# Hybrid attention, retention and ConvFFN layer on one core: early up-projection products re-ordered and placed in free half banks, reads and stores moved to other tiles and another queue

## The chip, the core and the metric

The kernel runs on one core of a Trainium2 chip. The metric is the time of one execution on the device in microseconds (us). Before the change three runs gave 1783.08, 1786.04 and 1786.34 us, median 1786.04. The engines are called as the profile calls them: PE is TensorE's matmul (PEld its weight load), DVE is VectorE, ACT is ScalarE, POOL is GpSimd and SP is SyncE, which here only issues DMAs. Each engine works its own instructions strictly in the order in which they stand; semaphores tie the engines together.

## The reference

One layer of a diffusion backbone over 1024 latent tokens of width 1024 and 256 context tokens. Attention and retention branches are merged and projected by `w_out` into a gated residual; a gated MLP with a depthwise convolution over tokens follows. The change touches the seam between the two:

```python
x = x + g1 * _merge(o_na, o_ret, xga, xgb, w_proj_na[l], w_proj_ret[l], w_out[l])
hx2 = _modulate(_rmsnorm(x, norm2_g[l]), sh2, sc2)
x = x + g2 * _conv_ffn(hx2, w_up[l], conv_w[l], conv_b[l], w_down[l])
...
return _rmsnorm(x, final_norm_g)

def _conv_ffn(h, w_up, conv_w, conv_b, w_down):
    u = h @ w_up
    ...
```

## The kernel before

**Precision.** Every float32 operand is split into a high and a low part (`split`, lines 85 to 87: a cast on ACT, then a subtraction on DVE), and a product is three matmuls: high with high, high with low, low with high (`open3`, L1374).

**Output projection.** `out_proj(tb)` makes the 128 tokens of one token block tb, 0 to 7: 48 matmuls into two PSUM tiles `om`, gate and residual on DVE (L1642, L1643), a store of the row block into `d_x1` (L1644), the squares on ACT (L1646), a scaling of their sum on DVE (L1647), a power on POOL (L1648) and the normed rows `xn` on DVE (L1649). `norm_out(tb)` transposes `xn` by 128-column pieces on TensorE (L1663), modulates them on ACT (L1670, L1673) and DVE (L1674, L1675). The normed tokens go into `h2`: the first half of the tokens into `h2a`, the second into `h2h` and `h2l`. For blocks 0 to 3 the modulated block `v` is also stored in `d_h` (L1677); for blocks 4 to 7 that store of the block 4 earlier is read back into `vo` (L1659), four differences are formed (L1681 to L1684) and, but for block 7, stored in `d_t` (L1689). Block 7's differences are split straight into the operands `T1` to `T4`.

**Up-projection.** It is a multiplication scheme with seven block products in place of eight (`Seven`). The weights of one unit n (one of 22) are the four blocks a11, a12, a21, a22, and POOL forms four sums of them, s1 to s4 (L1388 to L1391). The moving operands are halves of `h2` (B11, B21, B22) and the differences T1 to T4. Each unit has four half tiles of PSUM, each 128x512: `self.X`, `self.Y` and `self.Z` for the results, and a fourth, the second half of the tile z, that is not used. `u_tile` hands out tiles of two such halves.

**The seam.** Two units (`EARLY`) start before all tokens are normed. `early_plain(n)` makes a11 with B11 in X, copies X to p1 (L1718, on ACT), and adds a12 with B21 in X, which is C11, a block of the result. Then `norm_out(7)` follows, whose two transposed halves go into both halves of the tile z of unit 0, then reads of the twelve stored differences from `d_t` into `ur` tiles (`ur_load`, L1738) and their splits into T1 to T4. The `ur` tiles are twelve, and the weights `w_up` of all units and their sums s1 to s4 use the same twelve. `open` copies C11 out of X (`c11`, L1839, on ACT) and multiplies s4 with B22 into the same X; `close` makes the products with T1 to T4 and adds.

**What sets the order.** The text of the kernel gives the data flow; a scheduler lays each engine's instructions in a row. All loads of this stage, and all its stores, are issued on SP's queue. Tiles of a pool are handed on when their last reader is done. The pool `gates0` behind `gtile(0, ...)` has 17 tiles of 128x512, which held operands of the projections of the first token half; p1 and the other temporaries of the up-projection come from it.

Of the kernel before, what the change touches and what calls it, by code (L numbers as in the profile page):

```python
# [8 lines left out]
F32 = mybir.dt.float32  # L9
F32R = mybir.dt.float32r  # L10
AF = mybir.ActivationFunctionType
ALU = mybir.AluOpType
# [28 lines left out]
def tile_hybrid_layer(ctx, tc: tile.TileContext, io, dbg=None):  # L41
# [1519 lines left out]
    def gtile(half, dt, name):  # L1561
        return gpool[half].tile([P, 512], dt, tag="g", bufs=2 * KB + 1, name=name)
# [67 lines left out]
    def out_proj(tb):  # L1630
        half, ts = tb // 4, slice((tb % 4) * P, (tb % 4 + 1) * P)
        x1 = op.tile([P, D], F32, tag="x1", bufs=2, name="x1")
        xr = op.tile([P, D], F32, tag="xn", bufs=2, name="xn")
        sync.dma_start(x1, io["x"][tb * P : (tb + 1) * P])
        for dh in range(2):
            cs = slice(dh * 512, dh * 512 + 512)
            m = po.tile([P, 512], F32, tag="o", bufs=2, name="om")
            for kb in range(KB):
                wc = wo[kb, dh]
                h_, l_ = mg[kb, half]  # L1640
                mm3(m, h_[:, ts], l_[:, ts], wc[:, 0], wc[:, 1], kb == 0, kb == KB - 1)
            vec.tensor_tensor(xr[:, cs], m, gate1[:, cs], ALU.mult)  # L1642
            vec.tensor_tensor(x1[:, cs], xr[:, cs], x1[:, cs], ALU.add)  # L1643
        sync.dma_start(d_x1[tb * P : (tb + 1) * P], x1)  # L1644
        ss = op.tile([P, 2], F32, tag="ss", bufs=2, name="ss")
        act.activation(xr, x1, AF.Square, accum_out=ss[:, 0:1])  # L1646
        vec.tensor_scalar(ss[:, 0:1], ss[:, 0:1], 1.0 / D, EPS, ALU.mult, ALU.add)  # L1647
        pool.tensor_tensor(ss[:, 1:2], ss[:, 0:1], mhalf[:, 0:1], ALU.pow)  # L1648
        vec.tensor_scalar(xr, x1, ss[:, 1:2], None, ALU.mult)  # L1649
        return xr  # L1650

    def norm_out(tb, xr, banks=None):
        half, ts = tb // 4, slice((tb % 4) * P, (tb % 4 + 1) * P)
        if tb == 4:
            h2[1] = [None] * KH + [(gtile(0, F32R, "h2h"), gtile(0, F32R, "h2l")) for _ in range(KH)]
        vr = op.tile([P, KB, P], F32, tag="v", bufs=2, name="v")
        if half:
            vo = op.tile([P, KB, P], F32, tag="vo", bufs=1, name="vo")
            sync.dma_start(vo, d_h[tb - 4])  # L1659
        for kg in (1, 0):  # L1660
            tp = banks[kg].rearrange("p (k t) -> p k t", k=4) if banks else po.tile([P, 4, P], F32, tag="t", bufs=2, name="tp2")
            for k in range(4):
                pe.transpose(tp[:, k], xr[:, (kg * 4 + k) * P : (kg * 4 + k + 1) * P], ident)  # L1663
            for k in range(4):
                kb = kg * 4 + k
                t = h2[half][kb]
                a, sh = a2[:, kb : kb + 1], col[:, 24 + kb : 25 + kb]
                v = vr[:, kb]
                if t is None:
                    act.activation(v, tp[:, k], AF.Identity, bias=sh, scale=a)  # L1670
                    continue
                h_, l_ = (t[:, 0, ts], t[:, 1, ts]) if half == 0 else (t[0][:, ts], t[1][:, ts])
                act.activation(h_, tp[:, k], AF.Identity, bias=sh, scale=a)  # L1673
                vec.tensor_scalar(v, tp[:, k], a, sh, ALU.mult, ALU.add)  # L1674
                vec.tensor_tensor(l_, v, h_.bitcast(F32), ALU.subtract)  # L1675
        if half == 0:
            sync.dma_start(d_h[tb], vr)  # L1677
            return

        (b11, b21), (b12, b22) = [(t[:, :KH], t[:, KH:]) for t in (vo, vr)]  # L1680
        vec.tensor_tensor(b11, b12, b11, ALU.subtract)  # L1681
        vec.tensor_tensor(b12, b22, b12, ALU.subtract)
        vec.tensor_tensor(b22, b22, b11, ALU.subtract)
        vec.tensor_tensor(b21, b21, b22, ALU.subtract)  # L1684
        for c, t in enumerate((b11, b22, b12, b21)):
            if banks:
                split(combs[f"T{c + 1}"][0][:, tb - 4], combs[f"T{c + 1}"][1][:, tb - 4], t)
            else:
                sync.dma_start(d_t[c, tb - 4], t)  # L1689

    xr = None
    for tb in range(NTB):
# [12 lines left out]
    def early_bank(n):  # L1705
        return u_tile(2 * n), u_tile(2 * n + 1)

    def early_prod(bank, n, i):
        w = wload(io["w_up"][seq[n], 0, i])
        for k in range(KH):  # L1710
            x = h2[0][i * KH + k]
            open3(bank, w[:, 0, k * P : (k + 1) * P], w[:, 1, k * P : (k + 1) * P], x[:, 0], x[:, 1], i == 0 and k == 0, i == 1 and k == KH - 1)

    def early_plain(n):
        X = early[n][0][:, 0:512]
        early_prod(X, n, 0)
        p1 = gtile(0, F32, "pu")
        act.copy(p1, X)  # L1718
        early_prod(X, n, 1)
        return p1  # L1720

    early, early_p1, combs = [early_bank(0)], [], {}
    early_p1.append(early_plain(0))
    po.release()
    pu.append(ps("u_ps1", "left"))
    wop.release()
    gpool[1].release()
    early.append(early_bank(1))
    early_p1.append(early_plain(1))


    rp = sb("raws", "right")
# [3 lines left out]
    def ur_load(src):  # L1736
        t = rp.tile([P, 512], F32, tag="r", bufs=12, name="ur")
        sync.dma_start(t, src)  # L1738
        return t
# [47 lines left out]
    class Up(Seven):  # L1787
# [17 lines left out]
        def open(self):  # L1805
            self.banks()
            self.p1 = early_p1[self.n]
            self.c11()
            self.prod(self.X, self.s4, "B22", True, True)

        def close(self, n):
            if n == 0:
                self.prod(self.Z, self.s1, "T1", True, True)
            elif n == 1:
                self.u2, self.u3 = (self.tmp() for _ in range(2))
                self.prod(self.Y, self.s2, "T2", True, False)
                vec.tensor_tensor(self.u2, self.Y, self.p1, ALU.add)
                vec.tensor_tensor(self.u2, self.X, self.u2, ALU.add)
                self.add(0, 1, self.Z, self.u2)
            elif n == 2:  # L1820
                self.prod(self.Y, self.s3, "T3", False, False)
                vec.tensor_tensor(self.u3, self.Y, self.p1, ALU.add)
                self.add(1, 1, self.Z, self.u3)
            else:
                self.prod(self.Y, self.a22, "T4", False, True)
                self.add(1, 0, self.Y, self.p1)
# [31 lines left out]
    units[0].load()  # L1858
    for c in ("T1", "T2", "T3", "T4"):
        combs[c] = [tpl.tile([P, 4, KH, P], F32R, name=f"{c}{i}") for i in range(2)]  # L1860
    norm_out(NTB - 1, xr, (early[0][1][:, 0:512], early[0][1][:, 512:1024]))
    for c in (0, 1, 2, 3):
        hi, lo = combs[f"T{c + 1}"]
        for b in range(3):
            raw = ur_load(d_t[c, b])
            split(hi[:, b], lo[:, b], raw.rearrange("p (k t) -> p k t", k=KH))
    op.release()
    tap = sb("conv", "right")
# [252 lines left out]
```

## Time and profile before

| what | us |
|---|---|
| median of three runs | 1786.04 |
| the profiled execution's own time | 1782.43 |
| its span, from first to last instruction | 1780.0 |
| PE busy in the span | 1722.8 |
| DVE busy | 1309.6 |
| ACT busy | 853.6 |
| POOL busy | 581.7 |

All the profile's times are of the one profiled execution, which took 1782.43 us, and count from its first instruction. In a row of the timeline stand the start, how long it took, engine, line, operation, output and inputs and how many such instructions follow each other; in brackets, how long the engine stood idle before it and who ended the wait. A row of the waits has in total, times, longest. In rows of DMA issues stands the median time from issue to landing.

### The profile page before, as it was taken

What the parts mean: (1) busy time and instruction counts of PE and PEld (TensorE: products, weight loads), DVE (VectorE), ACT (ScalarE), POOL (GpSimd) and SP (SyncE); (2) the same over time, 40 slices, a digit from 0 to 9 for tenths busy, and PEclk for the clock granted to TensorE, in tenths of its full rate; (3) what the DMA queues carried; (4) which work ended last, traced back from release to release, by engine and by line L of the source; (5) the groups of instructions that cost most, each with busy time, mean ns of one, the idle gap of its engine ahead of it and who ended that gap; (6) DMA issues with size and microseconds to landing.
All of it is one profiled execution on the core that took longest, in us unless ns stands there. A gap on an engine that the chain in (4) does not pass through costs nothing.

```text
span 1780.0 us, 24636 instructions
## 1 busy us (share of the span) xinstructions
PE 1722.8 (97%) x8333; PEld 1427.2 (80%) x8333; DVE 1309.6 (74%) x2444; ACT 853.6 (48%) x1843; POOL 581.7 (33%) x485
## 2 busy tenths in 40 slices
PE   8799999999999999999999999699999999999997
PEld 3588888888888888788888888478888888788886
DVE  4978888765776766777664556789889989875755
ACT  4666666653443434443344334444444444554444
POOL 2510000002244343565413300346555555211444
PEclk9799999999999999999999999899999999999999
DMA  8133434433231212577658634522332333586754
GB/s 338 50 118 117 126 110 125 139 108 118 72 100 53 75 39 91 176 241 226 206 196 304 221 126 172 193 93 93 106 102 89 106 119 101 165 285 195 243 159 160
DMA packets 138973, 260.54 MB, mean 146 GB/s; under 512 B 15808, under 2 KB 28256, under 8 KB 138848
## 3 DMA queue, kind: packets, MB, share of 16 engines
q1 hardware_dynamic: 120928, 238.01, 40.9%
q10 hardware_dynamic: 17920, 20.98, 3.3%
q8 instruction: 65, 1.06, 0.2%
q14 instruction: 60, 0.49, 0.1%
HBM read 187.87 MB, written 68.44 MB: 144 GB/s over the span
## 4 chain that ended last, share of the span: by engine, by line
PE 44%; issue 5%; DVE 3%; POOL 3%; ACT 1%; DMA 1%; POOLq 0%; ACTq 0%; DVEq 0%; SPq 0%
PE u L1374 29%; PE y L1374 4%; PE om L121 2%; PE om L122 2%; PE om L123 2%; PE pr L111 2%; PE pr L110 2%; PE pr L112 2%; POOL x L1935 1%; PE pn L112 1%; PE pn L111 1%; PE pn L110 1%; DVE wc L87 1%; DVE ta L1763 0%; DVE at L1763 0%
## 5 line engine op out<-in xcount | busy, mean ns | idle before, releaser
L1374 PE MATMUL u<-T,wc 128*128 128x512 f32 x1056 | 248.5, 391 | 1.3 <-DVE pu L1416 0.8
L1374 PEld LDWEIGHTS u<-T,wc 128*128 128x128 f32 x1056 | 197.5, 188 | 46.1 <-ACT pu L1413 3.1
L1374 PE MATMUL y<-wc,ahl 128*128 128x512 f32 x924 | 210.6, 389 | 2.7 <-DVE wc L87 1.8
L1374 PEld LDWEIGHTS y<-wc,ahl 128*128 128x128 f32 x924 | 173.3, 188 | 39.6 <-DVE wc L87 2.5
L87 DVE TENSOR_TENSOR wc<-ur,wc 128x512 fp32r<-128x512 f32 x139 | 125.9, 908 | 65.0 <-ACT wc L86 65.0
L86 ACT CAST wc<-ur 128x512 fp32r<-128x512 f32 x139 | 86.3, 622 | 126.5 <-PE y L1374 72.0
L1374 PE MATMUL u<-h2a,wc 128*128 128x512 f32 x528 | 126.0, 393 | 4.1 <-ACT pu L1718 3.3
L111 PE MATMUL mm<-low,wc 128*128 128x512 f32 (+1 forms) x328 | 123.9, 378 | 0.0
L1374 PEld LDWEIGHTS u<-h2a,wc 128*128 128x128 f32 x528 | 99.7, 190 | 26.3 <-ACT pu L1718 3.7
L110 PE MATMUL mm<-hx,wc 128*128 128x512 f32 x264 | 107.4, 407 | 0.3 <-DVE vc L221 0.3
L112 PE MATMUL mm<-hx,wc 128*128 128x512 f32 x264 | 105.0, 398 | 0.0
L86 ACT CAST wc<-s 128x512 fp32r<-128x512 f32 x88 | 54.1, 621 | 103.7 <-PE u L1374 92.2
L87 DVE TENSOR_TENSOR wc<-s,wc 128x512 fp32r<-128x512 f32 x88 | 90.7, 1036 | 6.3 <-ACT wc L86 5.9
L1513 POOL TENSOR_TENSOR col<-col,bcol 128x32 f32<-128x32 f32 x1 | 0.2, 250 | 282.2 <-DVE aw L538 282.2
L123 PE MATMUL mm<-wc,low 128*128 128x512 f32 (+1 forms) x240 | 91.2, 380 | 0.0
L1374 PE MATMUL u<-hxT,wc 128*128 128x512 f32 x384 | 89.6, 389 | 0.0
L1374 PEld LDWEIGHTS u<-hxT,wc 128*128 128x128 f32 x384 | 72.1, 188 | 15.0
L87 DVE TENSOR_TENSOR wc<-raw,wc 128x512 fp32r<-128x512 f32 x88 | 66.1, 761 | 22.5 <-ACT wc L86 22.3
L121 PE MATMUL mm<-wc,hx 128*128 128x512 f32 x192 | 75.2, 392 | 0.6 <-ACT r L1105 0.6
L122 PE MATMUL mm<-wc,hx 128*128 128x512 f32 x192 | 75.2, 392 | 0.0
L1388 POOL TENSOR_TENSOR s<-ur 128x512 f32<-128x512 f32 x22 | 34.8, 1582 | 121.8 <-DVE wc L87 77.4
L1374 PE MATMUL u<-h2h,wc 128*128 128x512 f32 x176 | 60.9, 407 | 13.5 <-ACT uu L1839 9.7
(389 smaller groups left out, 4635.3 us busy)
## 6 DMA issues: line engine op xcount, KB each, us to landing
ur<-in_w_up SPq DMA_DIRECT2D x88, 256.0 KB, 2.8
ur<-d_a SPq DMA_DIRECT2D x77, 256.0 KB, 3.1
aw<-in_w_ada SPq DMA_DIRECT2D x32, 512.0 KB, 3.4
pj<-in_w_down SPq DMA_DIRECT2D x44, 256.0 KB, 4.7
d_w<-pj SPq DMA_DIRECT2D x44, 256.0 KB, 2.0
d_a<-sa SPq DMA_DIRECT2D x44, 256.0 KB, 2.0
ur<-d_w SPq DMA_DIRECT2D x44, 256.0 KB, 3.5
d_a<-at SPq DMA_DIRECT2D x33, 256.0 KB, 2.6
```

What stands on the lines that cost most here:

```text
L86: act.copy(hi, src)
L87: (lo_eng or vec).tensor_tensor(lo, src, hi.bitcast(F32), ALU.subtract)
L110: pe.matmul(out, wh, xh, start=k == 0, stop=False)
L111: pe.matmul(out, wh, xl, start=False, stop=False)
L112: pe.matmul(out, wl, xh, start=False, stop=k == n - 1)
L121: pe.matmul(out, ah, bh, start=first, stop=False)
L122: pe.matmul(out, ah, bl, start=False, stop=False)
L123: pe.matmul(out, al, bh, start=False, stop=last)
L1374: pe.matmul(out, a, b, start=first and n == 0, stop=last and n == 2, skip_group_check=True)
L1388: pin(pool.tensor_tensor(self.s1, self.a21, self.a22, ALU.add))
L1513: pool.tensor_tensor(col[:, 16:48], col[:, 16:48], bcol[:, 16:48], ALU.add)
L1935: pool.tensor_tensor(z, z, fg[:, gs(dh)], ALU.mult)
```

## The change

1. `d_x1`, `d_h` and `d_t` are stored by DMAs of ACT's queue instead of SP's.
2. `vo` becomes two half tiles from `gtile(0, ...)`, read by two DMAs of 256 KB instead of one of 512 KB.
3. `early_first(n)` makes only a11 with B11 and the copy to p1, for both units; the products of a12 with B21 follow in the program's text behind `norm_out(7)`.
4. `norm_out(7)` transposes into the first halves of the two units' tiles z, not into both halves of unit 0's.
5. `open` multiplies s4 with B22 into `self.W`, the idle second half of z, instead of X; `close` adds W instead of X.
6. The twelve reads of `d_t` go into tiles `tr` of `gtile(0, ...)` instead of `ur` tiles.

```diff
-        sync.dma_start(d_x1[tb * P : (tb + 1) * P], x1)
+        act.dma_start(d_x1[tb * P : (tb + 1) * P], x1)
...
         if half:
-            vo = op.tile([P, KB, P], F32, tag="vo", bufs=1, name="vo")
-            sync.dma_start(vo, d_h[tb - 4])
+            vo = [gtile(0, F32, "vo").rearrange("p (k t) -> p k t", k=KH) for _ in range(2)]
+            for i in range(2):
+                sync.dma_start(vo[i], d_h[tb - 4, :, i * KH : i * KH + KH])
...
-            sync.dma_start(d_h[tb], vr)
+            act.dma_start(d_h[tb], vr)
             return
-        (b11, b21), (b12, b22) = [(t[:, :KH], t[:, KH:]) for t in (vo, vr)]
+        (b11, b21), b12, b22 = vo, vr[:, :KH], vr[:, KH:]
...
-                sync.dma_start(d_t[c, tb - 4], t)
+                act.dma_start(d_t[c, tb - 4], t)
...
-    def early_plain(n):
-        X = early[n][0][:, 0:512]
-        early_prod(X, n, 0)
-        p1 = gtile(0, F32, "pu")
-        act.copy(p1, X)
-        early_prod(X, n, 1)
-        return p1
-
-    early, early_p1, combs = [early_bank(0)], [], {}
-    early_p1.append(early_plain(0))
+    def early_first(n):
+        early.append(early_bank(n))
+        early_prod(early[n][0][:, 0:512], n, 0)
+        early_p1.append(gtile(0, F32, "pu"))
+        act.copy(early_p1[n], early[n][0][:, 0:512])
+
+    early, early_p1, combs, traw = [], [], {}, {}
+    early_first(0)
     po.release()
     pu.append(ps("u_ps1", "left"))
     wop.release()
     gpool[1].release()
-    early.append(early_bank(1))
-    early_p1.append(early_plain(1))
+    early_first(1)
...
             self.p1 = early_p1[self.n]
             self.c11()
-            self.prod(self.X, self.s4, "B22", True, True)
+            self.W = early[self.n][1][:, 512:1024]
+            self.prod(self.W, self.s4, "B22", True, True)
...
-                vec.tensor_tensor(self.u2, self.X, self.u2, ALU.add)
+                vec.tensor_tensor(self.u2, self.W, self.u2, ALU.add)
...
-    norm_out(NTB - 1, xr, (early[0][1][:, 0:512], early[0][1][:, 512:1024]))
+    norm_out(NTB - 1, xr, (early[1][1][:, 0:512], early[0][1][:, 0:512]))
+    for n in range(EARLY):
+        early_prod(early[n][0][:, 0:512], n, 1)
     for c in (0, 1, 2, 3):
         hi, lo = combs[f"T{c + 1}"]
         for b in range(3):
-            raw = ur_load(d_t[c, b])
+            raw = gtile(0, F32, "tr")
+            sync.dma_start(raw, d_t[c, b])
```

Lines behind L1658 shift by one, the transposes from L1663 to L1664 and `ur_load` from L1738 to L1736. How the instructions then stand, at three places:

TensorE, from the last output projection on: 12 matmuls are one half product (`h2a` the moving half, `wc` the weights), four transposes of `xn` one half of block 7; - is the order before, + the order now.

```order
 L1374 MATMUL u<-h2a,wc 128x512 x12
-L1663 MATMUL u<-ident,xn 128x128 x4
-L1374 MATMUL u<-h2a,wc 128x512 x36
-L1663 MATMUL u<-ident,xn 128x128 x4
+L1664 MATMUL u<-ident,xn 128x128 x4
+L1374 MATMUL u<-h2a,wc 128x512 x17
+L1664 MATMUL u<-ident,xn 128x128 x4
+L1374 MATMUL u<-h2a,wc 128x512 x19
 L1374 MATMUL u<-h2h,wc 128x512
```

The first transposes keep their place behind 12 products. The second four stood behind all 48 and stand behind 29 now. Of the 17, five are unit 0's second half product and twelve unit 1's first; of the 19, seven end unit 0's and twelve are unit 1's second.

POOL at the same place, before: `ss` is the sum of squares of one block (L1648, the power), `s` the sums of one unit, the last `ss` row that of block 7.

```order
L1648 TENSOR_TENSOR ss_11717<-ss_11717,mhalf_81 128x1
L1648 TENSOR_TENSOR ss_11817<-ss_11817,mhalf_81 128x1
L1388 TENSOR_TENSOR s_11955<-ur_11947,ur_11949 128x512
L1389 TENSOR_TENSOR s_11956<-s_11955,ur_11951 128x512
L1390 TENSOR_TENSOR s_11957<-ur_11951,ur_11947 128x512
L1391 TENSOR_TENSOR s_11958<-ur_11953,s_11956 128x512
L1388 TENSOR_TENSOR s_12074<-ur_12066,ur_12068 128x512
```

And now:

```order
L1648 TENSOR_TENSOR ss_11719<-ss_11719,mhalf_81 128x1
L1388 TENSOR_TENSOR s_11927<-ur_11919,ur_11921 128x512
L1389 TENSOR_TENSOR s_11928<-s_11927,ur_11923 128x512
L1390 TENSOR_TENSOR s_11929<-ur_11923,ur_11919 128x512
L1648 TENSOR_TENSOR ss_11821<-ss_11821,mhalf_81 128x1
L1391 TENSOR_TENSOR s_11930<-ur_11925,s_11928 128x512
L1388 TENSOR_TENSOR s_12082<-ur_12074,ur_12076 128x512
```

Block 7's power has moved behind the first three sums of unit 0.

SP's queue, before, from the last stores of block 5's differences to the weights of unit 1 (`ur<-in_w_up` are weights, `ur<-d_t` differences read back):

```order
L1738 DMA ur<-in_w_up 128x512
L1659 DMA vo<-d_h 128x1024
L1644 DMA d_x_59<-x_11759 128x1024
L1738 DMA ur<-in_w_up 128x512 x2
L1689 DMA d_t<-vo 128x512
L1738 DMA ur<-in_w_up 128x512
L1689 DMA d_t<-v 128x512 x2
L1689 DMA d_t<-vo 128x512
L1738 DMA ur<-d_t 128x512 x3
L1659 DMA vo<-d_h 128x1024
L1738 DMA ur<-d_t 128x512 x9
```

And now (`tr` the differences read back):

```order
L1660 DMA vo<-d_h 128x512 x4
L1736 DMA ur<-in_w_up 128x512 x10
L1660 DMA vo<-d_h 128x512 x2
L1867 DMA tr<-d_t 128x512 x5
L1736 DMA ur<-in_w_up 128x512
L1867 DMA tr<-d_t 128x512
L1736 DMA ur<-in_w_up 128x512
L1872 DMA cw<-in_conv_w 128x132
L1874 DMA cb<-in_conv_b 128x44
L1867 DMA tr<-d_t 128x512 x6
```

The stores are gone from this queue; the weights of units 0 and 1 and two of unit 2's stand in one row ahead of the last read of `d_h` and of all reads of `d_t`.

## The prediction, made before the changed kernel ran

> **What bounds the kernel now.** I read the page's totals and its strip of 40 slices first: is one engine full, and where is it not?
>
> ```profile
> span 1780.0 us, 24636 instructions
> PE 1722.8 (97%) x8333; PEld 1427.2 (80%) x8333; DVE 1309.6 (74%) x2444; ACT 853.6 (48%) x1843; POOL 581.7 (33%) x485
> PE   8799999999999999999999999699999999999997
> ```
>
> TensorE (PE) is busy for 97% of the span; apart from both ends one slice, the 26th (about 1112 to 1157 us), stands at 6. That is the seam where the last output projections give way to the first up-projections, all that the change touches. The stages around it, by windows (the columns are length, then busy time of PE, PEld, DVE, ACT and POOL, granted clock, DMA share, GB/s):
>
> ```profile
> 1016.00:1108.00 92.00, 92.00 (x432) 76.71 (x431) 58.53 (x141) 30.40 (x67) 3.84 (x7) 1.00 0.43 151
> 1120.00:1130.00 10.00, 4.81 (x16) 3.71 (x16) 5.84 (x12) 4.79 (x11) 1.16 (x1) 0.83 0.78 262
> 1130.00:1150.00 20.00, 9.34 (x23) 6.87 (x24) 14.07 (x22) 11.12 (x21) 7.18 (x6) 0.66 0.55 189
> 1200.00:1300.00 100.00, 99.81 (x438) 81.76 (x437) 89.57 (x90) 45.20 (x62) 53.14 (x30) 1.00 0.30 99
> ```
>
> The stage before the seam and the one behind it have a full TensorE, so nothing is to be won or hidden there. In the seam it waits, and the granted clock falls. Its timeline names each wait in brackets:
>
> ```profile
> 1108.32 0.93 PE L1663 MATMUL tp<-ident,xn 128*128 128x128 f32 x7
> 1109.00 2.98 PE L1374 MATMUL u<-h2a,wc 128*128 128x512 f32 x12
> 1112.90 0.66 PE L1663 MATMUL u<-ident,xn 128*128 128x128 f32 x4 [0.92 <-DVE xn L1649]
> 1122.35 4.37 PE L1374 MATMUL u<-h2a,wc 128*128 128x512 f32 x12 [3.30 <-ACT pu L1718]
> 1126.56 0.60 PE L1663 MATMUL u<-ident,xn 128*128 128x128 f32 x4
> 1136.86 0.79 PE L1374 MATMUL u<-h2h,wc 128*128 128x512 f32 x1 [9.71 <-ACT uu L1839]
> 1141.72 0.63 PE L1374 MATMUL u<-h2h,wc 128*128 128x512 f32 x1
> 1146.14 0.79 PE L1374 MATMUL u<-h2h,wc 128*128 128x512 f32 x1 [3.79 <-ACT wc L86]
> 1150.64 15.57 PE L1374 MATMUL u<-T,wc 128*128 128x512 f32 x68
> 1166.59 3.72 PE L1374 MATMUL u<-T,wc 128*128 128x512 f32 x15 [0.38 <-DVE pu L1822]
> ```
>
> The waits are 0.92 + 3.30 + 9.71 + 3.79 = 17.7 us. At full rate one product costs 15.57 / 68 = 0.229 us. After the 3.30 us wait 12 products take 4.21 us up to 1126.56 instead of 2.75 (1.5 lost); after the 9.71 us wait 12 take 5.5 (2.7 lost); after the 3.79 us wait 13 take 4.5 up to 1150.64 instead of 3.0 (1.5 lost). The seam thus loses 17.7 + 5.7 = 23.4 us: the ceiling of any gain here.
>
> What stands behind the waits is read on ACT, POOL and SP:
>
> ```profile
> 1111.51 0.55 POOL L1648 TENSOR_TENSOR ss<-ss,mhalf 128x1 f32<-128x1 f32 x1 [11.28 <-DVE ss L1647]
> 1115.02 1.29 POOL L1388 TENSOR_TENSOR s<-ur 128x512 f32<-128x512 f32 x1 [2.96 <-issue]
> 1119.45 1.71 POOL L1391 TENSOR_TENSOR s<-ur,s 128x512 f32<-128x512 f32 x1
> 1140.39 1.27 POOL L1388 TENSOR_TENSOR s<-ur 128x512 f32<-128x512 f32 x1 [19.23 <-DMA ur<-in_w_up]
> 1121.19 0.62 ACT L86 CAST wc<-s 128x512 fp32r<-128x512 f32 x1 [2.02 <-POOL s L1391]
> 1121.71 0.58 ACT L1718 COPY pu<-u 128x512 f32<-128x512 f32 x1
> 1136.24 1.05 ACT L1839 COPY uu<-u 128x512 f32<-128x512 f32 x2
> 1145.47 3.21 ACT L86 CAST wc<-s 128x512 fp32r<-128x512 f32 x6 [7.29 <-POOL s L1391]
> 1107.17 0.39 SPq L1738 DMA_DIRECT2D ur<-in_w_up  x1
> 1114.17 0.42 SPq L1738 DMA_DIRECT2D ur<-in_w_up  x1
> 1118.43 1.97 SPq L1689 DMA_DIRECT2D d_t<-v  x2
> 1124.32 10.86 SPq L1738 DMA_DIRECT2D ur<-d_t  x9
> 1136.44 32.84 SPq L1738 DMA_DIRECT2D ur<-in_w_up  x13
> ```
>
> **Part by part.** *First products first.* The 3.30 us wait is for unit 1's copy out of PSUM (L1718, 0.58), which stood behind a cast that needed unit 0's fourth sum (1119.45). Now 12 products of unit 1 follow 5 of unit 0, then 4 transposes and 7 products of unit 0, and only then unit 1's second half: the copy has 7 × 0.229 = 1.6 us of cover for its 0.58. The wait and its 1.5 us of half rate go. If ACT were over 1 us behind, the rest would come back one for one.
>
> *Second half in idle half banks.* The 9.71 us wait is for the copy of C11 (L1839), behind fifteen casts of T that wait for reads of `d_t`. The s4 products now write another half bank and wait for no copy: 9.71 + 2.7 go. What is late next is s4's own weights: unit 0's fourth sum, cast and low part, which 48 products from the early halves cover.
>
> *Reads in the gates' tiles.* Before, unit 1's loads waited for `ur` buffers that the twelve reads of `d_t` held until 1136.44, so its sums began at 1140.39 and its cast at 1145.47: the 3.79 us wait and its 1.5. With other tiles for the reads, all eight loads of both units stand ahead of them; unit 1's sums follow unit 0's directly. If these tiles came free late, the reads alone would be late: between nothing and the T1 wait below.
>
> *Stores on ScalarE's queue.* 24 stores (8 `d_x1`, 4 `d_h`, 12 `d_t`) leave SP. An issue on ACT is priced by a row of another stage, and SP's time by its waits:
>
> ```profile
> 735.00 0.36 ACTq L1509 DMA_DIRECT2D d_pn<-pnt  x1
> SPq L1644 <- DVE v L1674: 17.5, 5, 5.8
> SPq L1689 <- DVE v L1682: 8.3, 3, 3.8
> SPq L1738 <- DVE wc L87: 20.6, 5, 13.2
> ur<-in_w_up SPq DMA_DIRECT2D x17, 256.0 KB, 3.4
> ```
>
> 24 × 0.36 = 8.6 us enter ACT, of which most falls in the 92 us where ACT works for 30.40: cost 0, at most 8.6 us if each issue held up a tile's evacuation, which the full TensorE there speaks against. The gain is that loads no longer stand behind stores that wait for VectorE (17.5 and 8.3 us): unit 0's fourth load went out at 1114.17, 7 us after its first. The Trainium skill, page "DMA: Bandwidth & Descriptors", section "Issuing engines are not separate DMA queues", says that issuing from several engines saves only the sequencer's time for issuing, since all run on the same 16 DMA engines. Read alone it makes this part worth nothing; SP's rows show another thing, in-order waits for data, and by them the part frees the loads.
>
> **What is late next.** *The power on POOL.* The last tile's L1648 feeds L1649 and so the transposes, 1.4 us later (1111.51 to 1112.90). It now stands behind three sums of unit 0, which took 1119.45 - 1115.02 = 4.4 us. They need two loads and buffers that TensorE frees by 1108.32. The first load goes out at 1107.17 at the latest and some 2.7 us sooner if nothing holds it, and lands 3.4 later: 1107.9 to 1110.6, so the first sum starts between 1108.4 and, if the second load lags by 1 us, 1111.5. I take 1109.4, near the middle: power at 1113.8, transposes at 1115.2 (1114.2 to 1117.3) instead of 1112.90. Nothing else can run on TensorE meanwhile: its 12 products end at 1112. That costs 2.3 us, and by the 3.30 us row 1.5 of half rate.
>
> From 1115.2 TensorE has 8 transposes (1.3), 60 products (13.7), the 1.5, and 2 first products of T1 (0.5): 1132.2.
>
> *T1's operand.* The last tile's differences need its `d_h` read, now behind two loads of unit 2 that wait for POOL's seventh sum.
>
> ```profile
> vo<-d_h SPq DMA_DIRECT2D x3, 512.0 KB, 3.6
> 1116.58 1.77 DVE L1682 TENSOR_TENSOR v<-v 128x512 f32<-128x512 f32 x1
> 1135.30 4.90 DVE L87 TENSOR_TENSOR T<-ur,T 128x512 fp32r<-128x512 f32 x8
> ```
>
> POOL is through the power at 1114.4, and four sums at 1.45 later it is 1120.2; four issues (some 1.4 us) and 3.6 of landing give 1125. VectorE then has 13 operations up to T1's last low part, 4.90 / 8 = 0.61 each undisturbed: 1133; I take 1134, with two disturbed by POOL. TensorE waits 1.8 us (0 to 5), with up to 1.5 of half rate, which I count in full. The 22 products left end at 1134 + 5.0 + 1.5 = 1140.5. Before, T1's last of 24 ended at 1150.64 + 23 × 0.229 = 1155.9. **Gain to there: 15.4 us.**
>
> Behind it VectorE has 14 more operations to the last operand of T4 (8.5 us, so 1142.5; with each slowed as at 1116.58, later than TensorE needs it): 0 to 5 us, I take 1.4. From 1200 on all repeats as before. **Sum: 14.0 us.** Against the profiled execution's 1782.43 us that is 1768.4; that execution lies 3.6 us below the median of 1786.04, and from the median it is 1772.0, which I give. The bounds together make a gain of 5 to 21 us, 1765 to 1781.
>
> **Rivals.** *VectorE takes TensorE's place.* L1682 took 1.77 us beside POOL's sums, and now eight sums run in a row beside its subtractions and splits. At some 1.1 us instead of 0.61 the 13 and 14 operations end 6 and then 13 us later, at 1140 and 1155.5, where T4 starts now at 1166.59: 11 us, less some 2 of waits on the way, is a gain of 9, 1777 us. For it: 89.57 of 100 us busy even in the steady stage. Against: POOL then waits for TensorE to give back buffers. The skill, page "SBUF — State Buffer", section "SBUF: two separate sides", says that a VectorE operation with two SBUF inputs and a GpSimd operation lock each other out for a whole instruction. The 1.77 agrees in size, about one POOL operation on top. Chance 0.17.
>
> *A short wait costs no half rate.* If the waits of 3.2 and 1.8 us leave the clock alone, 3 us less are lost: 1769. For it: 0.92 us cost none. Against: 3.30 us did. The skill's page "TensorE: Matmul & The Clock Gate", section "What's actually happening", asks for an idle window of about 3.4 us; the row of 3.30 goes the other way. Chance 0.05.
>
> *The gain is given back:* the reads of `d_t` wait for the gates' tiles or on the transfer engines (0.78 busy already at 1120), so T1 and T2 begin near 1150 as before: within 3 us, 1784. Against: the tiles belong to projections long done. The order of the instructions shows that the change does what it says, so that rival is part of this one. Chance 0.07.
>
> *Slower: the power waits for late loads.* TensorE has nothing ahead of the last transposes, so every microsecond that unit 0's first two loads land late is one of span. From a first sum at 1109.4 + 14 = 1123.4 on, the kernel is slower; at 1127 it takes 1790 us. For it: before, POOL began only at 1115.02, and a load on SP has waited for 13.2 us. Against: no store stands ahead of them now. Chance 0.07.
>
> **The numbers.** Forecast 0.64 at 1768 to 1776, and the four rivals as above. I predict 1772.0; 1765 to 1781 holds the forecast and the rivals with a gain, some 8 in 10. A measurement of this kernel tells 0.2% (3.6 us) from no change: faster 0.86, same 0.07, slower 0.07.
>
> **What would show it.** TensorE's waits for `pu` L1718 and `uu` L1839 must be gone; POOL's L1648 must stand behind three sums, with a wait of 2 to 4 us for `xn` before the transposes; T1's start must lie near 1134, released by VectorE. A `u` product that waits for a load, or a seam past 1150 us, would make the forecast wrong.

## The result and the profile after

Four runs of the changed kernel gave 1772.24 to 1775.33 us, median 1774.61, against 1785.91 for the kernel before beside them: ratio 0.9938, 95% interval 0.9921 to 0.9955. That is faster by 11.3 us, where 14.0 were predicted. The two profiled executions, 1782.43 and 1775.33 us, differ by 7.1 us only: the one before lies 3.5 us below its median, the one after 0.7 above. The page of the profiled execution (1775.33 us), its span, totals and strip of 40 slices:

```profile
span 1773.2 us, 24636 instructions
PE 1724.2 (97%) x8333; PEld 1428.0 (81%) x8333; DVE 1312.6 (74%) x2444; ACT 854.8 (48%) x1843; POOL 581.5 (33%) x485
PE   8799999999999999999999999799999999999997
```

The 26th slice has gone from 6 to 7; PE's total work is nearly the same. By windows, columns as before:

```profile
1016.00:1108.00 92.00, 92.00 (x432) 76.72 (x431) 58.65 (x141) 31.96 (x70) 3.84 (x7) 1.00 0.42 152
1130.00:1150.00 20.00, 17.48 (x69) 13.71 (x68) 19.54 (x26) 14.98 (x28) 6.31 (x4) 0.91 0.61 200
1200.00:1300.00 100.00, 99.83 (x433) 81.80 (x432) 87.88 (x89) 44.97 (x62) 48.98 (x28) 0.98 0.28 93
```

The stage ahead of the seam stays as it was. Behind it, from 1200 to 1300 us, PE makes 433 products instead of 438, at a granted clock of 0.98 instead of 1.00; more on that below. Between 1130 and 1150 PE works for 17.48 us instead of 9.34, and now DVE is full (19.54 of 20). PE's timeline of the seam and of what follows shows which waits went and which stayed; lines behind L1659 have moved by one or two (L1663 is now L1664, L1718 is L1719, L1822 is L1821):

```profile
1109.21 1.03 PE L1664 MATMUL tp<-ident,xn 128*128 128x128 f32 x8
1118.84 1.12 PE L1664 MATMUL u<-ident,xn 128*128 128x128 f32 x4 [5.85 <-DVE xn L1649]
1119.61 5.44 PE L1374 MATMUL u<-h2a,wc 128*128 128x512 f32 x17
1127.83 3.03 PE L1374 MATMUL u<-h2a,wc 128*128 128x512 f32 x12 [0.72 <-ACT pu L1719]
1138.92 10.04 PE L1374 MATMUL u<-T,wc 128*128 128x512 f32 x36 [2.17 <-DVE T L87]
1156.78 4.59 PE L1374 MATMUL u<-T,wc 128*128 128x512 f32 x19 [0.62 <-DVE pu L1821]
1161.21 2.88 PE L1374 MATMUL u<-h2a,wc 128*128 128x512 f32 x12
...
1199.61 4.38 PE L1374 MATMUL u<-h2a,wc 128*128 128x512 f32 x12 [2.04 <-DVE pu L1422]
...
1231.28 0.39 PE L1374 MATMUL u<-h2h,wc 128*128 128x512 f32 x1
```

The waits for C11's copy (9.71) and for unit 1's cast (3.79) are gone, that for unit 1's first copy is 0.72 instead of 3.30. In their place PE stands 5.85 us ahead of the last transposes, 2.17 ahead of T1's operand and, behind the seam, 2.04 for DVE.

**Two measures of the seam.** The code ahead of the seam is the same in all these kernels, yet the seam began between 1103.61 and 1110.51 us in their profiled executions: spans of single executions can't rank changes of 2 or 3 us. So the seam is measured from the last eight transposes into `tp` to unit 2's first 12 products. In the kernel before these two rows of PE's timeline, and a third that is used below, are:

```profile
1108.21 1.03 PE L1663 MATMUL tp<-ident,xn 128*128 128x128 f32 x8
...
1170.14 2.88 PE L1374 MATMUL u<-h2a,wc 128*128 128x512 f32 x12
...
1237.04 0.39 PE L1374 MATMUL u<-h2h,wc 128*128 128x512 f32 x1
```

1170.14 - 1108.21 = 61.93 us before, 1161.21 - 1109.21 = 52.00 after: 9.9 us.

This measure ends too early, since PE waits once more behind unit 2's first products: 0.78 us in the kernel before, 0.40 and 2.04 after (the 2.04 with 12 products in 4.38 us instead of 2.75 behind it), and nothing in some of the kernels below. Each unit has one block of products with `h2h` and `h2l`. From the third such block behind the seam on, all the kernels run alike (541.9 to 544.3 us to the end of the span). The second measure goes from the same start to that block, over the same products in every kernel: 1237.04 - 1108.21 = 128.83 us before, 1231.28 - 1109.21 = 122.07 after. That is a gain of 6.8 us, close to the 7.1 by which the two executions differ; so 3.2 of the 9.9 us are lost again behind the seam.

Each kernel stands here with one profiled execution, so differences under 1 us are not read. All runs (a: first products first; b: the idle half banks; c: reads in the gates' tiles; d: stores on ACT's queue; e in the expectations is the power on POOL):

| kernel | seam from, to | seam | to third block | median | ratio to before, 95% interval |
|---|---|---|---|---|---|
| before | 1108.21, 1170.14 | 61.93 | 128.83 | 1785.91 | |
| a, b, c, d: the change | 1109.21, 1161.21 | 52.00 | 122.07 | 1774.61 | 0.9938 (0.9921 to 0.9955) |
| without a | 1108.46, 1159.99 | 51.53 | 121.51 | 1775.06 | 0.9947 (0.9932 to 0.9961) |
| without b | 1107.03, 1161.80 | 54.77 | 121.62 | 1774.74 | 0.9950 (0.9934 to 0.9966) |
| without c | 1106.69, 1169.89 | 63.20 | 130.10 | 1782.29 | 0.9992 (0.9981 to 1.0003) |
| without d | 1103.61, 1162.33 | 58.72 | 125.80 | 1778.65 | 0.9977 (0.9962 to 0.9993) |
| c, d only | 1109.51, 1166.69 | 57.18 | 124.03 | 1777.63 | 0.9964 (0.9954 to 0.9975) |
| a, b only | 1107.33, 1168.48 | 61.15 | 128.14 | 1780.69 | 0.9990 (0.9980 to 1.0001) |
| change + power first | not read | | | 1776.19 | 0.9953 (0.9938 to 0.9967) |
| change + d_h read first | 1108.45, 1160.64 | 52.19 | 117.53 | 1770.55 | 0.9928 (0.9913 to 0.9944) |
| change + both | 1108.56, 1159.41 | 50.85 | 116.19 | 1769.50 | 0.9925 (0.9910 to 0.9941) |
| both, sums behind L1649 | 1110.51, 1161.70 | 51.19 | 116.53 | 1772.29 | 0.9938 (0.9923 to 0.9952) |
| both, four stores on SP | 1108.69, 1163.38 | 54.69 | 126.87 | 1778.82 | 0.9976 (0.9965 to 0.9987) |
| both, sums mostly filled | 1107.85, 1156.16 | 48.31 | 113.59 | 1766.96 | 0.9895 (0.9879 to 0.9912) |

The profiled execution of the kernel with the power first ran at less than half pace from end to end (span 3701.1 us), so its seam is not read; the overlong executions (two there, one with a and b only) are left out of the ratios, though not of the medians.

The medians stand beside different runs of the kernel before, whose medians were 1782.78 to 1785.91 us. Rows are therefore compared by the ratio, and where two intervals overlap the times alone tell nothing.

### The profile page after: what moved, and what is told of

The parts are those of the page before. It is cut to its first block, busy times and chain, and to the rows that moved or that the text cites. A ratio compares the mean times of both kernels' runs of the same rounds, so it can differ in the third digit from the quotient of the medians.

```text
span 1773.2 us, 24636 instructions
## 1 busy us (share of the span) xinstructions
PE 1724.2 (97%) x8333; PEld 1428.0 (81%) x8333; DVE 1312.6 (74%) x2444; ACT 854.8 (48%) x1843; POOL 581.5 (33%) x485
## 4 chain that ended last, share of the span: by engine, by line
PE 44%; issue 5%; DVE 4%; POOL 3%; ACT 1%; DMA 1%; POOLq 0%; ACTq 0%; DVEq 0%; SPq 0%
PE u L1374 29%; PE y L1374 4%; PE pr L111 2%; PE pr L110 2%; PE pr L112 2%; PE om L123 2%; PE om L122 2%; PE om L121 2%; DVE wc L87 1%; POOL x L1937 1%; PE pn L112 1%; PE pn L111 1%; PE pn L110 1%; POOL pd L1974 0%; DVE at L1761 0%
## 5 line engine op out<-in xcount | busy, mean ns | idle before, releaser
L87 DVE TENSOR_TENSOR wc<-wr,wc 128x512 fp32r<-128x512 f32 x56 | 55.9, 1001 | 22.4 <-ACT wc L86 20.2
```

The source lines that it names most:

```text
L87: (lo_eng or vec).tensor_tensor(lo, src, hi.bitcast(F32), ALU.subtract)
```

## The experiments

### One part undone at a time

```diff
  without a, in early_first:
         act.copy(early_p1[n], early[n][0][:, 0:512])
+        early_prod(early[n][0][:, 0:512], n, 1)
  (and not behind norm_out(7))
  without b, in open:
-            self.W = early[self.n][1][:, 512:1024]
+            self.W = self.X
  without c, at the reads of d_t:
-            raw = gtile(0, F32, "tr")
-            sync.dma_start(raw, d_t[c, b])
+            raw = ur_load(d_t[c, b])
  without d, three times:
-        act.dma_start(...)
+        sync.dma_start(...)
```

Expected without a, b, c and d:

> The changed kernel with the old order of the early products: unit 0's second half right behind its first, unit 1's first products only behind them. Theory (step a of the prediction, the wait for unit 1's copy out of PSUM comes back when its products come late): TensorE waits again for pu of L1719, 2 to 5 us with the half rate behind it, and the span is 2 to 5 us above the changed kernel's 1773.2. Rival (the wait before the last transposes and the one before T1 hide it): the span is within 1.5 us of 1773.2, and what is lost at the copy is taken off the wait for T1's operand.

> The changed kernel with the s4 products of units 0 and 1 written again into the half bank of C11, so that they wait for its copy on ScalarE. Theory (step b): the copy L1838 stands behind the casts of T that wait for reads of d_t; in the changed kernel it ran at 1137.2, and TensorE came to the s4 products near 1130.9, so a wait of some 6 us and some 2 of half rate come back: span 1778 to 1783. Rival: since the reads of d_t no longer wait for ur buffers, the copy is on time, and the span is within 2 us of 1773.2.

> The changed kernel with the twelve reads of d_t in ur buffers again, unit 1's loads behind them. Theory (step c): unit 1's sums begin only when the casts and low parts of T have given the buffers back, TensorE waits for wc of s4 or s1 of unit 1 for 3 to 8 us: span 1776 to 1782. Rival: VectorE's work on T ends the seam anyway, and unit 1's late weights fall into that wait: span within 2 us of 1773.2.

> The changed kernel with all 24 stores on SyncE's queue again. It has a side effect: the last tile's power then stands ahead of unit 0's sums on GpSimd, as before the change. Theory (steps d and e are opposite and of one size): the wait of 5.85 us before the last transposes shrinks to 1 us, unit 1's loads are late behind the stores of d_t, and TensorE waits 3 to 6 us for unit 1's s4 weights: span 1771 to 1777. Rival 1 (in-order loads are worth more than the power's place): over 1778. Rival 2 (the stores' place is worth nothing, only the power counts): 1766 to 1769.

Measured: without a the seam is 51.53, no longer than with it, and the wait for unit 1's copy is 1.00 us; it was not taken off the wait for T1's operand, which is 2.51. Without b it is 54.77, 2.8 more. In PE's timeline without b the s4 products do wait for C11's copy, though hardly by that name, since two products of T stand just ahead:

```profile
1132.80 1.22 PE L1374 MATMUL u<-T,wc 128*128 128x512 f32 x2 [4.56 <-ACT T L86]
1135.06 0.80 PE L1374 MATMUL u<-h2h,wc 128*128 128x512 f32 x1 [1.04 <-ACT uu L1838]
```

These are the 5.6 us that were expected; but T1 to T4 then run almost without a gap behind it, so that half is given back, and the rest behind the seam: to the third block it is 121.62, not longer than with b. In both cases the rival came true by the profiled spans (1774.0 and 1771.4), though not by its reason: without b the copy was late. To the third block neither a nor b, undone alone, costs anything. Without c the theory held, and by more than expected: 63.20 (130.10 to the third block, 8.0 more), and PE waits three times for unit 1's weights:

```profile
1133.17 0.79 PE L1374 MATMUL u<-h2h,wc 128*128 128x512 f32 x1 [6.13 <-ACT wc L86]
1138.05 1.22 PE L1374 MATMUL u<-h2h,wc 128*128 128x512 f32 x2 [3.66 <-DVE wc L87]
1144.48 0.79 PE L1374 MATMUL u<-h2h,wc 128*128 128x512 f32 x1 [1.80 <-ACT wc L86]
```

Without d the profiled span (1772.4) lies in the theory's range, but by chance: that execution entered the seam 5.6 us sooner than the changed kernel's. By seam (58.72) and median (1778.65) it is the first rival: the stores' place is worth 6.7 us in the seam and 3.7 to the third block, although the power stands ahead of the sums again and the wait for `xn` is 1.91 us instead of 5.85. PE's wait, and what SP did meanwhile:

```profile
1137.97 0.80 PE L1374 MATMUL u<-h2h,wc 128*128 128x512 f32 x1 [16.01 <-ACT wc L86]
```

```profile
1115.36 0.38 SPq L1736 DMA_DIRECT2D ur<-in_w_up  x1
1115.84 0.40 SPq L1690 DMA_DIRECT2D d_t<-v  x1
1116.63 0.33 SPq L1690 DMA_DIRECT2D d_t<-vo  x1
1117.01 0.97 SPq L1660 DMA_DIRECT2D vo<-d_h  x2
1118.02 7.26 SPq L1867 DMA_DIRECT2D tr<-d_t  x6
1125.32 0.43 SPq L1736 DMA_DIRECT2D ur<-in_w_up  x1
```

Unit 1's third load goes out at 1125.32, behind stores that waited for DVE and behind six reads.

### Two parts alone

The kernel with c and d only has the diffs of "without a" and "without b" together; the one with a and b only those of "without c" and "without d".

> The kernel before with only the reads of d_t in the gates' tiles and the stores on ScalarE's queue (and d_h read in two halves): the old order of the early products and the s4 products in the half bank of C11 stay. Theory (the copies of unit 1's first product and of C11 were late only because ScalarE stood on casts whose data came late; with the data on time both waits are small, whatever the order): seam 51 to 56, against 61.9 before and 52.0 with all parts. Rival (each of the two orders was free to undo only because the other one stood): seam 58 or more.

> The kernel before with only the first products first and the s4 products in the idle half bank (with its d_h tiles): reads of d_t in ur buffers and all stores on SyncE's queue, as before. Theory (unit 1's loads stand behind the twelve reads, so its s4 weights come near 35 us into the seam, as before): both copies' waits go and come back as one long wait for wc of unit 1: seam 59 to 63. Rival (the prediction's sum, where these two parts are worth 3.3 + 1.5 and 9.7 + 2.7 us): seam 45 to 55.

Measured: 57.18 and 61.15. a and b alone do nothing (0.8 us): one wait of 17.8 us for unit 1's weights takes the place of both copies' waits, as the theory had it. c and d alone give 4.8 us by either measure (of 9.9 and of 6.8), a miss between theory and rival: with the old orders PE still waits 1.78 us for `pu`, 4.30 for T and 2.12 for `uu`. So loads on time are the condition. On top of them, and to the third block, a alone adds 2.4 us (124.03 to 121.62), b alone 2.5 (121.51) and both together 2.0 (122.07): one of the two is enough.

### What holds the seam now

Two edits on top of the change, each alone and both: the power of block 7 ahead of unit 0's sums, and its read of `d_h` ahead of unit 2's loads. `tc.issue_after(x)` keeps what it encloses behind x on x's engine.

```diff
+        seam["power"] = pool.tensor_tensor(ss[:, 1:2], ss[:, 0:1], mhalf[:, 0:1], ALU.pow)
...
-    units[0].load()
+    with tc.issue_after(seam["power"].ins):
+        units[0].load()
...
+                seam["read"] = sync.dma_start(vo[i], d_h[tb - 4, :, i * KH : i * KH + KH])
...
+            with tc.issue_after(seam["read"].ins):
+                units[i].load()
             units[i].step(0)
```

> The changed kernel with the last tile's power ahead of unit 0's sums on GpSimd; nothing else moves but what follows from that. The seam is measured from the last eight transposes of the out projection's banks to unit 2's first products (52.0 us in the changed kernel). Theory (the read of d_h for the last tile, issued at 1124.72 behind two loads of unit 2 that wait for GpSimd's seventh sum, now sets T1's start): the wait before the last transposes falls from 5.85 to 1 to 2 us, most of it comes back as a longer wait for T1's operand, seam 49.5 to 51.5. Rival (the wait before the transposes is what bounds the seam, as the prediction has it): it goes in full with its half rate, seam 45.5 to 47.

> The changed kernel with the last tile's read of d_h ahead of unit 2's loads on SyncE's queue; the power stays behind three sums. Theory: the read lands some 8 us sooner, but the last transposes still start near 10 us into the seam, so T1's operand gains at most the 2.2 us that TensorE waits for it now: seam 50 to 52. Rival (the late read alone sets T1's start): seam 48 to 49.5.

> Both: the power ahead of unit 0's sums, and the last tile's read of d_h ahead of unit 2's loads. Theory (each of the two waits hides the other, so only both together pay): the wait before the transposes is 1 to 2.5 us, T1's start moves forward by 5 us or more, seam 44.5 to 47.5, and the median some 5 us below the changed kernel's. Rival (VectorE's low parts of T bound T1 whatever comes before): seam 49.5 to 52, with the wait now for T of L87.

> As with both, but unit 0's first sum waits for VectorE's scaling of the last tile (L1649), so that no sum on GpSimd runs beside it. Theory (the scaling took 1.74 us beside a sum and 0.75 alone, so the two block each other): L1649 is back at 0.75 and the transposes start about 1 us sooner than with both edits alone, while the sums come 0.7 us later at no cost: seam 0.5 to 1.5 us shorter. Rival (the 1.74 was not from the sum beside it): L1649 stays over 1.2 us, and the seam is equal or longer.

Measured: the read alone gives 52.19, no gain in the seam: the wait for T1's operand falls from 2.17 to 0.55 us, as the theory said, and comes back as later waits for DVE. But with it PE has no wait at all behind the seam, and to the third block the time is 117.53, 4.5 less than the changed kernel's. Neither theory nor rival had that gain. The edit also moves unit 2's loads, and which of the two takes the waits behind the seam away is not shown; the times (ratio 0.9928 against 0.9938) are too near to tell. The power alone shows no gain in time (ratio 0.9953), and as its seam is not read, theory and rival stay undecided.

Both together give 50.85 and not 44.5 to 47.5. That theory fell: T1 starts 27.4 us into the seam, 2.3 sooner and not 5. The rival's range holds the seam, but not its reason, since T1 starts without a wait. To the third block both give 116.19, 5.9 less than the changed kernel, of which the read alone gives 4.5. In the kernel with both, PE's timeline:

```profile
1114.47 0.66 PE L1664 MATMUL u<-ident,xn 128*128 128x128 f32 x4 [2.14 <-DVE xn L1649]
1126.28 4.43 PE L1374 MATMUL u<-h2a,wc 128*128 128x512 f32 x12 [3.59 <-ACT pu L1719]
1144.52 4.91 PE L1374 MATMUL u<-T,wc 128*128 128x512 f32 x20 [1.55 <-DVE wc L87]
```

The transposes come 5.9 us into the seam instead of 9.6, and 3.59 us are lost again at unit 1's copy. What ACT did ahead of that copy, and DVE ahead of ACT:

```profile
1120.64 3.27 ACTq L1690 DMA_DIRECT2D d_t<-v  x2
1123.96 0.46 ACT L1674 ACTIVATE h2h<-u,col,a 128x128 fp32r<-128x128 f32 x1 [4.15 <-DVE v L1675]
1125.64 0.58 ACT L1719 COPY pu<-u 128x512 f32<-128x512 f32 x1 [1.22 <-DVE h2l L1676]
```

```profile
1112.67 1.74 DVE L1649 TENSOR_SCALAR xn<-x,ss 128x1024 f32<-128x1024 f32 x1 [0.73 <-POOL ss L1648]
1116.03 1.36 DVE L1676 TENSOR_TENSOR h2l<-v,h2h 128x128 fp32r<-128x128 f32 x1
1121.79 1.76 DVE L1684 TENSOR_TENSOR v<-v,vo 128x512 f32<-128x512 f32 x1
```

ACT stands on the stores of `d_t` and on a modulation, both of which wait for DVE, and most of DVE's subtractions take two to five times as long as elsewhere (0.28 and 0.68 us) while POOL's eight sums run. With the sums held back until L1649 is done, that one operation is short again (0.75) and the transposes start 4.9 us into the seam, 1.0 sooner as expected; but then PE waits 6.54 us for the copy, and of the 0.5 to 1.5 us expected nothing is gained (51.19):

```profile
1114.59 0.75 DVE L1649 TENSOR_SCALAR xn<-x,ss 128x1024 f32<-128x1024 f32 x1 [0.73 <-POOL ss L1648]
```

Next, ACT's part of it or DVE's? With both edits, the four stores of block 6 go back to SP:

```diff
-                act.dma_start(d_t[c, tb - 4], t)
+                (sync if tb == NTB - 2 else act).dma_start(d_t[c, tb - 4], t)
```

> As with both the power and the read of d_h first, and the second last tile's four stores of d_t on SyncE's queue, so that ScalarE doesn't stand on stores that wait for VectorE's subtractions ahead of unit 1's copy (there two issues held it for 3.27 us and the copy ran at 1125.64, 6 us after its products). Theory: the wait of 3.59 us for the copy shrinks to 0.5 to 2 us, seam 47.5 to 49.5. Rival (VectorE, slowed by the sums beside it, is what everything in the seam waits for): the wait moves to T of L87 or to wc, seam 50 to 52.

Measured: 54.69, worse than with both and outside both ranges. On ACT, just ahead of the copy (L1719, at 1125.60), and on SP:

```profile
1125.24 0.46 ACT L1674 ACTIVATE h2h<-u,col,a 128x128 fp32r<-128x128 f32 x1 [4.09 <-DVE v L1675]
```

```profile
1126.58 0.32 SPq L1690 DMA_DIRECT2D d_t<-vo  x1
1126.95 0.93 SPq L1660 DMA_DIRECT2D vo<-d_h  x2
```

The copy ran at the same time into the seam (16.9 us; 17.1 with both), since ACT still stood on a modulation that waits for DVE: the stores on ACT were not what held it. And the read of `d_h` now stands behind stores that wait for DVE (1126.95 instead of 1115.46 to 1119.95), so T1 begins 29.5 us into the seam instead of 27.4. Behind the seam PE waits again, and to the third block it is 126.87, 10.7 more than with both.

The last run takes most of DVE's slowness away and leaves the order of PE, ACT, DVE and SP as it was:

```diff
+            for s in (self.s1, self.s2, self.s3, self.s4)[: 0 if n == 512 else 4]:
+                pool.memset(s[:, n:512], 0.0)
-            pin(pool.tensor_tensor(self.s1, self.a21, self.a22, ALU.add))
+            pin(pool.tensor_tensor(self.s1[:, :n], self.a21[:, :n], self.a22[:, :n], ALU.add))
...
-        units[0].load()
+        units[0].load(n=32)
```

> As with both the power and the read of d_h first, but of the eight sums of units 0 and 1 on GpSimd only the first 32 of 512 columns are computed and the rest is filled with zeros (so the up projections of these two units are left wrong); PE, ACT, DVE and SP issue the same instructions in the same order. Theory (VectorE is what the seam waits for, and it is slow because a two-input sum on GpSimd and a VectorE operation on SBUF block each other): L1649, L1676 and L1682 to L1685 of the last two tiles take 0.28 to 0.75 us instead of 1.4 to 1.8, unit 1's copy runs 3 to 5 us sooner after the transposes than in the run with both (11.2 us), its wait falls from 3.59 to under 1 us, and the seam is 44 to 47.5 against 50.9. Rival (VectorE is slow by the number of its operations, or fills block it as sums do): the copy's wait stays over 2.5 us and the seam at 49 to 52.

Measured: 48.31, 2.5 us less than with both (2.6 to the third block), 0.8 beyond the theory's range. The copy comes 7.1 us behind the transposes instead of 11.2, as soon as PE has made its input, and PE no longer waits for it. The subtractions are back at 0.28 to 0.74 us. L1649 (here L1651) is not: it ran beside four fills.

```profile
1111.94 2.27 DVE L1651 TENSOR_SCALAR xn<-x,ss 128x1024 f32<-128x1024 f32 x1 [0.73 <-POOL ss L1650]
1115.74 0.29 DVE L1678 TENSOR_TENSOR h2l<-v,h2h 128x128 fp32r<-128x128 f32 x1
1118.03 0.74 DVE L1686 TENSOR_TENSOR v<-v,vo 128x512 f32<-128x512 f32 x1
```

What is left is DVE. The windows of whole seams, of the kernel before, after, with both, and with the fills, in this order:

```profile
1108.21:1170.14 61.93, 43.83 (x173) 34.37 (x172) 46.61 (x68) 29.06 (x55) 24.07 (x17) 0.86 0.49 164
```

```profile
1109.21:1161.21 52.00, 42.28 (x174) 32.89 (x172) 45.15 (x67) 27.87 (x54) 21.65 (x17) 0.90 0.58 188
```

```profile
1108.56:1159.41 50.85, 42.39 (x174) 32.46 (x172) 47.74 (x68) 27.35 (x54) 27.70 (x17) 0.93 0.59 193
```

```profile
1107.85:1156.16 48.31, 41.44 (x174) 31.52 (x172) 44.21 (x68) 27.13 (x54) 19.93 (x25) 0.96 0.64 203
```

The third column of times is DVE: busy for 75% of the seam before, 87% after, 94% with both edits; PE's own work is shorter. DVE's 44 to 48 us are no fixed floor, since they hold the time by which POOL's operations lengthen DVE's: the run with fills takes 3.5 us off DVE's busy time and 2.5 off the seam. How much of the 44 us that are left could still go is not shown.

## Why the prediction was right, point by point

- **The mechanism.** The waits named in the seam went or shrank, the power came to stand behind three sums, and T1's start is released by DVE, as said. The time, 1774.61, is 2.6 us above the forecast, inside the range. Three of the named signs came out otherwise: the wait for `xn` is 5.85 us and not 2 to 4, 0.72 are left of the wait for `pu`, and T1 resumed at 1138.92 and not near 1134.
- **The size.** Between the two profiled executions the gain is 7.1 us, half of the 14.0. The medians' 11.3 came nearer to the forecast because the profiled execution before lies 3.5 us below its median; as far as the traces show, that nearness is partly luck. To the third block 6.8 of the 14.0 came. Of the 7.2 that are missing, 3.6 were lost up to T1's end, 0.5 from there to the seam's end, and 3.2 behind the seam, which the prediction put at nothing ("From 1200 on all repeats as before").
- **A term that was mis-sized: the power on POOL.** The step took the first sum at 1109.4 (1108.4 to 1111.5), 1.2 us behind the start of the last eight transposes into `tp` (1108.21; the prediction's row x7 at 1108.32 is without the first of them). POOL's and DVE's timelines after:

```profile
1112.67 1.27 POOL L1388 TENSOR_TENSOR s<-ur 128x512 f32<-128x512 f32 x1 [11.18 <-DMA ur<-in_w_up]
1116.45 0.55 POOL L1648 TENSOR_TENSOR ss<-ss,mhalf 128x1 f32<-128x1 f32 x1
```

```profile
1112.42 0.15 DVE L1647 TENSOR_SCALAR ss<-ss 128x1 f32<-128x1 f32 x1 [0.94 <-ACT xn L1646]
1117.04 1.74 DVE L1649 TENSOR_SCALAR xn<-x,ss 128x1024 f32<-128x1024 f32 x1 [3.86 <-POOL ss L1648]
```

  The transposes came 9.6 us into the seam and not 7.0 (1115.2 - 1108.21): the sum began 3.5 us in, 2.3 later than taken, three sums took 3.8 instead of 4.4, and L1649 took 1.74 instead of 0.75. That makes 2.6 us. The first load was out in time, at 1106.00, and landed in 2.7 us; the second went out at 1107.13 and took 5.4, and POOL's first sum waited for it. DMA issues from 1103 to 1114 after, and from 1103 to 1119 before:

```profile
q1 hardware_dynamic: 660, 1.21, 37.7%
q10 hardware_dynamic: 591, 1.15, 27.8%
...
ur<-in_w_up SPq DMA_DIRECT2D x7, 256.0 KB, 5.4
```

```profile
q1 hardware_dynamic: 1549, 3.34, 61.6%
...
ur<-in_w_up SPq DMA_DIRECT2D x4, 256.0 KB, 3.7
```

  A load took 5.4 us to land instead of 3.7 (medians; 3.4 was taken): the stores, now on a queue of their own, move 1.15 MB at the same time as the loads. The other kernels agree: 5.4 again with c and d only (1103 to 1114), 3.1 without d, where the stores are on SP's queue (1096 to 1110). Where the stores left SP, though, the loads also go out in longer rows there, and no run separates the two causes.
- **a, 4.8 us, and b, 12.4 us.** Undone alone, neither costs anything to the third block; undone together they cost 2.0 us, and without c and d they gain 0.7. Both copies stood behind casts whose data came late; c and d bring the data on time, and then the copies are nearly on time too. The four waits were priced as if each had a cause of its own.
- **c, 5.3 us, and d, nothing by itself:** undone alone they cost 11.2 and 6.7 in the seam, 8.0 and 3.7 to the third block; alone they give 4.8 of the 6.8. They are the condition for all the rest. The Trainium skill, page "DMA: Bandwidth & Descriptors", section "Issuing engines are not separate DMA queues", by which d would be worth little more than issue time, does not hold here for the total: with the in-order waits on SP, d was worth 6.7 us in the seam and 3.7 to the third block. That all queues share the same engines is in keeping with the 5.4 us.
- **T1's operand** was taken ready 25.8 us into the seam (1134 - 1108.21); T1 resumed at 29.7 with a wait of 2.17 (1.8 predicted). Of the 3.9 us, 2.6 are those above, 0.7 the wait left at unit 1's copy and 0.4 this wait.
- **Behind T1** 1.4 us were taken for DVE, at most 5. From T1's end to the seam's end 2.0 were lost (a gain of 11.9 to T1's end, by 22 of the 36 products at 10.04 / 36 us each, and 9.9 in all), and behind the seam 3.2 more.
- **The rivals.** "VectorE takes TensorE's place" priced a gain of 9 us, 1777 in time. PE's later waits in the rows above, 2.17 at T1, 0.62 behind it and 2.04 behind the seam, are all for DVE, which is busy for 87% of the seam. The measured 1774.61 lies as near to 1777 as to the forecast's 1772.0, and the stated range held both: the time does not choose between them, and the waits say that the rival had much of it right. "A short wait costs no half rate" fell: both half rates came. Behind the 5.85 us wait 17 products took 5.44 us, where 15.57 / 68 each make 3.9; behind the 2.17 us wait the granted clock was 0.59 from 1138.92 to 1142.00, and 36 products took 10.04 us instead of 8.2. Yet not every such wait costs: behind 1.91 us for `xn` the clock was 0.56 with a and b only (1113.0 to 1116.5) and 1.00 without d (1109.3 to 1114.5).

## What to carry to other kernels

Waits that follow each other in one stage can have one cause, as here: look at what the engine named as releaser itself was waiting for, and count the root once, not each wait. When stores leave an in-order queue, price both what they held up there and what they now move beside. Ask of every freed wait which engine the next one will be for: here it was VectorE, busy for 87% of the seam after the change. And measure up to the point from which the kernels run alike: 3.2 us of the gain were lost behind the seam, and the edit that puts the read of `d_h` first showed its 4.5 us only there.

## What the runs showed of the hardware

- A scaling of 128x1024 on DVE with a single SBUF operand (L1649) took 0.75 us alone, 1.74 beside a sum on POOL and 2.27 beside four fills on POOL; a subtraction of two SBUF operands of 128x128 took 0.28 alone, 1.36 beside sums and 0.29 beside fills. The Trainium skill, page "SBUF — State Buffer", section "SBUF: two separate sides", says that DVE and GpSimd lock each other out where the DVE operation is in a mode that uses both ports, whatever GpSimd does, or has two SBUF inputs while GpSimd reads SBUF. The runs agree on the second half; on the first they fit, if this scaling is in such a mode, which no run shows.
- The step from `tp` by DVE (L1675, 128x128 out of PSUM) stayed at 0.39 to 0.41 us beside sums and fills alike.
